# Two Strassen stages of a Hymba step on one Trainium2 core: weight forms and block splits spread between the products

## The chip, the cores and the metric

The kernel runs on one core of a Trainium2 chip. The metric is the device time of one execution in microseconds, the median of several runs. The engines are named as the profile names them: PE (TensorE), DVE (VectorE), ACT (ScalarE), POOL (GpSimd) and SP (SyncE, which here only issues DMAs).

## What is computed

One layer of a decoder: a mixer (gMLP gating beside sliding-window attention), an output projection, and a feed-forward network, over 1024 prompt rows and 32 sample rows of width 1024, all in fp32. The change lies in the feed-forward network, whose hidden width is 4096:

```python
h = rms_norm(x, g_pre_ffn)
f = jnp.einsum('bsf,fd->bsd', jnp.square(jax.nn.relu(jnp.einsum('bsd,df->bsf', h, w_up))), w_down)
return x + rms_norm(f, g_post_ffn)
```

## The kernel before

Every fp32 matrix product is made of three matmuls on a high and a low part of each operand. `split` (L126) makes the parts: ACT casts to fp32r (L128, the high part), DVE subtracts (L129, the low part). A weight that is split lies in a `unit()`, one of 16 buffers.

Both products of the network are Strassen-Winograd products: seven products in place of eight, on sums and differences of blocks. The seven weight operands, the forms, are made by `up_weights` (L888) from two raw loads of 512 KB: four sums on DVE (L900, L901, L904, L906) and seven splits, ten jobs in all, for both stages.

The **up stage** (from about 371 to 750 us) has 16 pairs p of column blocks of the weight, and two groups g of rows (272 and 256 wide). Each (p,g) is a `Quad` (L774) of seven products of twelve matmuls. A turn of the loop at L1062 takes the next quad q and the one before, prev: `q.first()` (products 1 and 2), `prev.third()` (products 4 and 3, then relu, square and four sums on DVE), `prev.stores()` (seven blocks to the DRAM tensor f_d, issued on SP through `load`), then, where prev ends a pair, the raw loads of pair prev.p + 2 and all ten of its weight jobs, and at last `q.second()` (products 6, 5, 7). Products 1, 6, 7, 4 add up in one PSUM bank, A; between them ACT copies A out (`snap`, L801), and the next one waits for that copy. DVE adds the copies to the other banks: L822 or L829 with product 2, L837 with product 7's snap, L844 with product 3. `fo` is the result buffer of a quad (four in the pool `fop`), and is free again when its stores have landed. The raw up weights `rw` have one pair of buffers (`rawp`).

The **down stage** (752 to 1146 us) has eight rounds r of four steps, (r,0,0), (r,0,1), (r,1,0), (r,1,1), for the weight half c and the row group g (L1108). A step makes products 1, 5, 6, 2, 7, 3, 4, each on two banks of PSUM. Products 1, 6, 7, 4 add up in A; ACT copies A to other banks after products 1 and 6 (`fork`, L1130), and after product 5 (D), 2 (C), 7 (E), 3 (B) and 4 (A) `gather` (L1120) adds the banks to accumulators `accD`, `accC`, `accE`, `accB`, `accA`: copies by ACT in r = 0 (L1124), adds by DVE after (L1126). Product 4 goes on in the bank that the gather into accE reads. Blocks come back from f_d by `f_load` (L1039): six loads and splits for each set. Before step (r,0,0) the program has all ten weight jobs of (r,1,.) and the six block splits of the next round's g = 0, before (r,1,0) ten weight jobs, before (r,1,1) six splits.

After that, `combine` (L1209) adds accD to accB and accE for each row group, and `Finish` (L1161) transposes, scales and stores the output.

PE's and SP's order is that of the program. ACT, DVE and POOL are ordered by the scheduler, by its own priorities, and each engine then works through its list in that order; buffers of a pool are reused in turn, and who takes one waits for the last reader of its former content.

Of the kernel before, what the change touches and what calls it, by code (L numbers as in the profile page):

```python
# [8 lines left out]
F32 = mybir.dt.float32  # L9
# [36 lines left out]
def hymba_step(ctx: ExitStack, tc: tile.TileContext, a: dict):  # L46
# [813 lines left out]
    with ExitStack() as pcx:  # L860
# [27 lines left out]
        def up_weights(raws):  # L888
# [3 lines left out]
            def form(src):  # L892
                w = unit()
                split(w[:, 0], w[:, 1], src)
                return w

            ws = {1: form(b11), 2: form(b21)}
            t13 = unit().bitcast(F32)
            t24 = unit().bitcast(F32)
            vec.tensor_tensor(t13[:, 0], b12, b11, ALU.subtract)  # L900
            vec.tensor_tensor(t24[:, 0], b22, t13[:, 0], ALU.subtract)  # L901
            ws[6] = form(t24[:, 0])
            ws[5] = form(t13[:, 0])
            vec.tensor_tensor(t13[:, 1], b22, b12, ALU.subtract)  # L904
            ws[7] = form(t13[:, 1])
            vec.tensor_tensor(t24[:, 1], b21, t24[:, 0], ALU.subtract)  # L906
            ws[4] = form(t24[:, 1])
            ws[3] = form(b22)
            return ws
# [129 lines left out]
    def f_load(fs, pool_=None):  # L1039
        tiles, r, g = fs  # L1040
        n = SUB[g]
        for a0, a1 in ((0, 2), (2, 4), (4, 7)):
            for f, p in zip(tiles, (2 * r, 2 * r + 1)):
                raw = (pool_ or stage).tile([P, D], F32, name="raw")[:, 0:(a1 - a0) * n].rearrange("p (i c) -> p i c", c=n)
                load(raw, f_d[p][g][:, a0:a1])
                split(f[:, a0:a1, 0], f[:, a0:a1, 1], raw)
        return tiles

    def down_weights(r, c, tiles):
        for i, t in enumerate(tiles):  # L1050
            load(t, a["w_down"][2 * r + c, i])
        return up_weights(tiles)
# [9 lines left out]
    prev = q0  # L1062
    for i, (p, g) in enumerate(seq):
        q = Quad(p, g, ws_up[p])
        q.first()
        prev.third()
        flush()
        prev.stores()
        if prev.g == 1:
            del ws_up[prev.p]  # L1070
            if prev.p + 2 < NPAIR:
                ws_up[prev.p + 2] = up_weights(up_raws(prev.p + 2))
# [4 lines left out]
        if i == len(seq) - 2:  # L1077
# [3 lines left out]
            fs0 = f_load(f_tiles(0, 0, 0))  # L1081
        if i == len(seq) - 1:
            wdn0 = down_weights(0, 0, stage_raws())
        q.second()
        prev = q
# [6 lines left out]
    with ExitStack() as pf:  # L1092
# [3 lines left out]
        frp = pf.enter_context(tc.tile_pool(name="frp", bufs=2, reuse_waits="tile"))  # L1096
        rp = pf.enter_context(tc.tile_pool(name="rp", bufs=2, reuse_waits="tile"))
# [10 lines left out]
        def step(r, c, g, fs, ws, inserts=(), renewed=()):  # L1108
            n = SUB[g]
            A, D_, C, B = [[b[:, 0:n] for b in banks[2 * i:2 * i + 2]] for i in range(4)]  # L1110

# [20 lines left out]
            ins = dict(inserts)  # L1132

# [5 lines left out]
            if 0 in renewed:  # L1139
                renew(banks[6:8], ws[1])  # L1140
            fork(C)
            product(5, D_, True)
            gather("D", D_)
            insert(0, 6)
            product(6, A, False)
            if 1 in renewed:
                renew(banks[6:8], ws[1])
            fork(B)
            product(2, C, False)
            gather("C", C)  # L1150
            insert(1, 2)
            product(7, A, False)
            gather("E", A)
            product(3, B, False)
            gather("B", B)
            insert(2, 4)
            product(4, A, False)
            gather("A", A)
            banks[:] = banks[2:4] + banks[0:2] + banks[6:8] + banks[4:6]

        class Finish:  # L1161
# [7 lines left out]
            def half(self, h, bank):  # L1169
                r, t = self.r, self.t  # L1170
                hs = slice(h * 512, (h + 1) * 512)
                if t == NCH:
                    av = rp.tile([P, 4, NS], F32, name="av")
# [7 lines left out]
                junk = rp.tile([P, 512], BF16, name="rl")  # L1181
# [27 lines left out]
        def combine(g):  # L1209
            for k in "BE":  # L1210
                vec.tensor_tensor(gacc(k, g), gacc(k, g), gacc("D", g), ALU.add)  # L1211

        renew(banks[4:8], wdn0[1])
        f_cur = [fs0, f_load(f_tiles(0, 0, 1), frp)]
        w_cur = [wdn0]
        sets = 2
        for r in range(NR):
            f_nxt, w_nxt = [], []

            def prefetch(g):  # L1220
                nonlocal sets
                if r + 1 < NR:
                    f_nxt.append(f_load(f_tiles(0 if sets % 3 < 2 else 1, r + 1, g), frp))
                    sets += 1

            if r + 1 < NR:
                w_cur.append(down_weights(r, 1, stage_raws()))
                prefetch(0)
                step(r, 0, 0, f_cur[0], w_cur[0])
                step(r, 0, 1, f_cur[1], w_cur[0])  # L1230
                w_nxt.append(down_weights(r + 1, 0, stage_raws()))
                step(r, 1, 0, f_cur[0], w_cur[1])
                prefetch(1)
                step(r, 1, 1, f_cur[1], w_cur[1])
            else:
                w_cur.append(down_weights(r, 1, stage_raws()))
                step(r, 0, 0, f_cur[0], w_cur[0])
# [7 lines left out]
                step(r, 1, 0, f_cur[0], w_cur[1])  # L1245
# [119 lines left out]
```

## Time and profile before

| what | value |
| --- | --- |
| three runs | 1163.37, 1170.16 and 1171.62 us, median 1170.16 |
| profiled execution | 1167.12 us |
| its span, first to last instruction | 1165.4 us |
| busy: PE, PE weight loads, DVE, ACT, POOL | 1060.0, 982.7, 833.1, 531.7, 50.8 us |
| mean granted TensorE clock | 0.967 |
| HBM | 126 GB/s over the span |

The span is what the trace covers; the execution's time has 1.7 us around it. An engine's idle time just before an instruction is put down to what ended it, its releaser. A granted clock of 1.00 is 2.4 GHz, 0.50 is 1.2 GHz.

### The profile page before, as it was taken

Reading aid. Unit: us, or ns where it says so; the run is one execution under the profiler, and the core shown is the slowest. Engines: PE = TensorE matmul, PEld = TensorE weight load, DVE = VectorE, ACT = ScalarE, POOL = GpSimd, SP = SyncE. Lnnn points to the kernel's source line nnn. Section 1 sums busy time; section 2 is a strip of 40 time slices with the busy share of each in tenths; the row PEclk is TensorE's granted clock in tenths of the full one; section 3 lists DMA queues with packets and bytes.
Section 4 is the critical chain, followed back from the end, with each engine's and each line's share of the span. In section 5 each row is a group of like instructions: output and inputs, shape, how many; then the busy total and the mean of one; then the engine's idle time right before and its main releaser. Section 6 shows DMA issues by size and latency. Waiting matters only on the chain. (4 is left out here: it accounts for less than half of the span.)

```text
span 1165.4 us, 19447 instructions
## 1 busy us (share of the span) xinstructions
PE 1060.0 (91%) x7443; PEld 982.7 (84%) x7443; DVE 833.1 (71%) x1707; ACT 531.7 (46%) x1184; POOL 50.8 (4%) x77
## 2 busy tenths in 40 slices
PE   7999999999999989999989898899789889898894
PEld 5888777887878979989989897889789889898894
DVE  6678868776678857657665665746877877878657
ACT  6587956664445323223223322367443544444322
POOL 2000003101010000000000000000000000000001
PEclk9999999999999989999999898999899999999997
DMA  8332211245333243343344333645353332533516
GB/s 275 122 100 73 91 38 34 80 154 172 127 109 127 82 140 108 132 140 135 112 139 152 107 127 106 208 144 171 104 187 108 111 127 95 186 101 103 175 39 220
DMA packets 76077, 147.42 MB, mean 127 GB/s; under 512 B 10048, under 2 KB 40224, under 8 KB 75968
## 3 DMA queue, kind: packets, MB, share of 16 engines
q1 hardware_dynamic: 70176, 132.72, 34.8%
q10 hardware_dynamic: 5808, 13.47, 3.0%
q8 instruction: 58, 0.95, 0.3%
q14 instruction: 35, 0.29, 0.1%
HBM read 102.41 MB, written 44.79 MB: 126 GB/s over the span
## 5 line engine op out<-in xcount | busy, mean ns | idle before, releaser
L64 PE MATMUL z<-f,w 128*128 128x272 f32 (+1 forms) x1920 | 263.5, 295 | 39.4 <-DVE accE L1126 21.6
L64 PEld LDWEIGHTS z<-f,w 128*128 128x128 f32 x1920 | 252.2, 198 | 45.0 <-DVE accE L1126 23.0
L64 PE MATMUL z<-w,hT_hi 128*128 128x512 f32 (+1 forms) x768 | 210.2, 380 | 0.4 <-DVE raw L192 0.4
L64 PE MATMUL z<-hT_hi,w 128*128 128x272 f32 (+1 forms) x768 | 153.5, 294 | 11.9 <-ACT w L128 11.3
L64 PEld LDWEIGHTS z<-w,hT_hi 128*128 128x128 f32 x768 | 133.8, 188 | 25.2 <-DVE raw L192 0.8
L64 PEld LDWEIGHTS z<-hT_hi,w 128*128 128x128 f32 x768 | 127.7, 198 | 13.1 <-ACT w L128 11.8
L64 PE MATMUL z<-sg,w 128*128 128x272 f32 (+1 forms) x768 | 109.6, 294 | 17.8 <-ACT s L801 17.7
L64 PE MATMUL z<-w,hT_lo 128*128 128x512 f32 (+1 forms) x384 | 124.5, 378 | 0.0
L64 PEld LDWEIGHTS z<-sg,w 128*128 128x128 f32 x768 | 102.0, 196 | 19.6 <-ACT s L801 19.1
L64 PE MATMUL z<-hT_lo,w 128*128 128x272 f32 (+1 forms) x384 | 112.5, 293 | 0.0
L128 ACT CAST f<-raw 128x544 fp32r<-128x544 f32 (+3 forms) x96 | 67.3, 707 | 96.5 <-DMA raw<-f_d 65.7
L129 DVE TENSOR_TENSOR f<-raw,f 128x544 fp32r<-128x544 f32 (+3 forms) x96 | 75.2, 795 | 42.0 <-ACT f L128 41.6
L64 PE MATMUL t<-f,w 128*128 128x272 f32 (+1 forms) x768 | 104.1, 285 | 0.0
L801 ACT COPY s<-z 128x256 f32<-128x256 f32 (+1 forms) x93 | 35.0, 377 | 143.5 <-PE z L64 133.7
L64 PEld LDWEIGHTS t<-f,w 128*128 128x128 f32 x768 | 97.9, 189 | 0.0
L128 ACT CAST w<-w 128x512 fp32r<-128x512 f32 x128 | 71.0, 617 | 51.2 <-DVE w L901 46.2
L129 DVE TENSOR_TENSOR w<-w 128x512 fp32r<-128x512 f32 x128 | 80.3, 683 | 0.2 <-ACT w L128 0.2
L64 PEld LDWEIGHTS z<-w,hT_lo 128*128 128x128 f32 x384 | 67.6, 188 | 14.0
L1130 ACT COPY t<-z 128x256 f32<-128x256 f32 (+1 forms) x128 | 46.6, 366 | 68.1 <-PE z L64 64.8
L64 PEld LDWEIGHTS z<-hT_lo,w 128*128 128x128 f32 x384 | 76.1, 198 | 0.0
L772 DVE SCALAR_TENSOR_TENSOR fo<-fo 128x544 f32<-128x544 f32 (+1 forms) x64 | 44.9, 702 | 22.1 <-ACT fo L841 21.7
L64 PE MATMUL t<-sg,w 128*128 128x272 f32 (+1 forms) x384 | 52.9, 287 | 1.1 <-DVE fo L822 0.6
(255 smaller groups left out, 1581.7 us busy)
## 6 DMA issues: line engine op xcount, KB each, us to landing
raw<-in_w_down_dram SPq DMA_DIRECT2D x32, 512.0 KB, 5.8
rw<-in_w_up_dram SPq DMA_DIRECT2D x28, 512.0 KB
f_d<-fo SPq DMA_DIRECT2D x64, 136.0 KB, 1.8
raw<-f_d SPq DMA_DIRECT2D x32, 272.0 KB, 3.2
f_d<-fo SPq DMA_DIRECT2D x64, 128.0 KB, 1.8
raw<-f_d SPq DMA_DIRECT2D x32, 256.0 KB
f_d<-raw SPq DMA_DIRECT2D x48, 136.0 KB, 1.8
raw<-f_d SPq DMA_DIRECT2D x16, 408.0 KB, 3.3
```

The source lines that it names most:

```text
L64: tc.keep_in_program_order(pe.matmul(out, lhsT, rhs, start=start, stop=stop, skip_group_check=resumed))
L128: pin(act.copy(hi, src))
L129: pin(vec.tensor_tensor(lo, src, hi.bitcast(F32), ALU.subtract))
L772: vec.scalar_tensor_tensor(f, f, 0.0, f, ALU.max, ALU.mult)
L801: act.copy(s, self.A)
L1130: act.copy(dst[j], A[j])
```

## The change

It does five things. (1) `up_weights` becomes `weight_jobs`, a list of ten jobs (form 1, first sums, form 2, sum, form 6, form 5, sum, form 7, form 4, form 3), and the up loop runs two of them after `q.first()`, two before `q.second()` and two after it. (2) The raw loads of a pair are issued one quad earlier, and ahead of the seven stores of that turn. (3) In the down stage block fetches, block splits and weight jobs are spread over seven slots (`background`) of each step. (4) The raw block buffers `fr` of the down stage are four in place of two. (5) `combine(1)` is cut in two halves, one ahead of the last step.

```diff
-            ws = {1: form(b11), 2: form(b21)}
...
+            return [lambda: form(1, b11), t12, lambda: form(2, b21), t4, lambda: form(6, lambda: tmp["b"][:, 0]),
+                    lambda: form(5, lambda: tmp["a"][:, 0]), t3, lambda: form(7, lambda: tmp["a"][:, 1]),
+                    lambda: form(4, lambda: tmp["b"][:, 1]), lambda: form(3, b22)]
...
+    raws = {2: up_raws(2)}
+    jobs = []
+
+    def work(k):
+        for job in jobs[:k]:
+            job()
+        del jobs[:k]
+
     for i, (p, g) in enumerate(seq):
         q = Quad(p, g, ws_up[p])
         q.first()
+        work(2)
         prev.third()
         flush()
-        prev.stores()
         if prev.g == 1:
             del ws_up[prev.p]
             if prev.p + 2 < NPAIR:
-                ws_up[prev.p + 2] = up_weights(up_raws(prev.p + 2))
+                ws_up[prev.p + 2] = {}
+                jobs += weight_jobs(raws.pop(prev.p + 2), ws_up[prev.p + 2])
+        elif prev.p + 2 < NPAIR and prev.p > 0:
+            raws[prev.p + 2] = up_raws(prev.p + 2)
+        prev.stores()
...
+        work(2)
         q.second()
+        work(2)
         prev = q
...
-        frp = pf.enter_context(tc.tile_pool(name="frp", bufs=2, reuse_waits="tile"))
-        rp = pf.enter_context(tc.tile_pool(name="rp", bufs=2, reuse_waits="tile"))
+        frp = pf.enter_context(tc.tile_pool(name="frp", bufs=4, reuse_waits="tile"))
+        avp = pf.enter_context(tc.tile_pool(name="avp", bufs=2, reuse_waits="tile"))
...
+            def background(i):
+                nonlocal done
+                k = len(jobs) * (i + 1) // 7
+                for job in jobs[done:k]:
+                    job()
+                done = k
...
-                w_cur.append(down_weights(r, 1, stage_raws()))
-                prefetch(0)
-                step(r, 0, 0, f_cur[0], w_cur[0])
-                step(r, 0, 1, f_cur[1], w_cur[0])
-                w_nxt.append(down_weights(r + 1, 0, stage_raws()))
-                step(r, 1, 0, f_cur[0], w_cur[1])
-                prefetch(1)
-                step(r, 1, 1, f_cur[1], w_cur[1])
...
+                step(r, 0, 0, f_cur[0][0], w_cur[0], mix(first, wj[:5]) + fetches(g0[:3]))
+                step(r, 0, 1, f_cur[1][0], w_cur[0],
+                     mix(splits(g0[:3]), wj[5:]) + fetches(g0[3:]) + [wload(r + 1, 0)])
+                wj = weight_jobs(wraw, w_nxt[0])
+                step(r, 1, 0, f_cur[0][0], w_cur[1], mix(splits(g0[3:]), wj[:5]) + fetches(g1[:3]))
+                step(r, 1, 1, f_cur[1][0], w_cur[1],
+                     mix(splits(g1[:3]), wj[5:]) + fetches(g1[3:]) + [wload(r + 1, 1)])
+                late = g1[3:]
...
-        combine(1)
+                combine(1, 0, 2)
+                step(r, 1, 1, f_cur[1][0], w_cur[1], (), [(0, finish(2)), (1, finish(3)), (2, finish(NCH))], True)
+        combine(1, 2, 4)
```

Here `first` is `late`, the last three block splits of the current round's g = 1 (with more in r = 0), `wj` the ten jobs of the next weights, and `mix` takes from two lists in turn.

SP at the start of the up stage, before: the stores of a turn (f_d0_1 is pair 0, g = 1), then the raw loads of pair 2 (rw_4558, rw_4559).

```order
L51 DMA f_d1_0_100<-fo_4223 128x272
L51 DMA f_d0_1_99<-fo_4376 128x256
L51 DMA f_d0_1_99<-raw_4546 128x256 x2
L51 DMA f_d0_1_99<-fo_4377 128x256
L51 DMA f_d0_1_99<-raw_4546 128x256
L51 DMA f_d0_1_99<-fo_4376 128x256
L51 DMA f_d0_1_99<-fo_4377 128x256
L51 DMA rw_4558<-in_w_up_dram 128x1024
L51 DMA rw_4559<-in_w_up_dram 128x1024
L51 DMA f_d1_1_101<-fo_4489 128x256
```

The same place after (rw_4442 and rw_4443 are the raw loads of pair 3):

```order
L51 DMA f_d0_0_98<-fo_4189 128x272
L51 DMA rw_4442<-in_w_up_dram 128x1024
L51 DMA rw_4443<-in_w_up_dram 128x1024
L51 DMA f_d1_0_100<-fo_4226 128x272
L51 DMA f_d1_0_100<-raw_4437 128x272 x2
L51 DMA f_d1_0_100<-fo_4227 128x272
L51 DMA f_d1_0_100<-raw_4437 128x272
L51 DMA f_d1_0_100<-fo_4226 128x272
L51 DMA f_d1_0_100<-fo_4227 128x272
L51 DMA f_d0_1_99<-fo_4380 128x256
```

The loads of pair 3 have moved ahead of the stores of quad (1,0); pair 2's stand still further ahead.

DVE at the same place, before: the last row of post-processing of quad (0,1) (L852), product 7's add of quad (1,1) (L837), then the jobs of pair 2.

```order
L852 TENSOR_TENSOR fo_4376<-fo_4377,raw_4546 128x256
L837 TENSOR_TENSOR fo_4490<-t_4488,s_4627 128x256
L129 TENSOR_TENSOR w_4562<-rw_4558,w_4562 128x512
L129 TENSOR_TENSOR w_4565<-rw_4558,w_4565 128x512
L900 TENSOR_TENSOR w_4568<-rw_4559,rw_4558 128x512
L904 TENSOR_TENSOR w_4568<-rw_4559 128x512
L901 TENSOR_TENSOR w_4569<-rw_4559,w_4568 128x512
```

And after: w_4744 is form 3 of pair 2, the rows from w_4779 on are jobs of pair 3, and L829 and L837 belong to quad (1,1).

```order
L129 TENSOR_TENSOR w_4741<-w_4570,w_4741 128x512
L852 TENSOR_TENSOR fo_4380<-fo_4381,raw_4554 128x256
L129 TENSOR_TENSOR w_4744<-rw_4220,w_4744 128x512
L129 TENSOR_TENSOR w_4779<-rw_4442,w_4779 128x512
L900 TENSOR_TENSOR w_4782<-rw_4443,rw_4442 128x512
L904 TENSOR_TENSOR w_4782<-rw_4443 128x512
L901 TENSOR_TENSOR w_4783<-rw_4443,w_4782 128x512
L129 TENSOR_TENSOR w_4830<-rw_4442,w_4830 128x512
L907 TENSOR_TENSOR w_4783<-rw_4442,w_4783 128x512
L129 TENSOR_TENSOR w_4875<-w_4783,w_4875 128x512
L829 TENSOR_TENSOR fo_4497<-z_4495,s_4511 128x256
L837 TENSOR_TENSOR fo_4498<-t_4496,s_4611 128x256
```

The jobs of pair 2 have moved up into the work of the quad before, and jobs of pair 3, which need rw_4442 and rw_4443, now stand ahead of L829 and L837 of quad (1,1).

DVE in a step (r,0,0) of the down stage, before: the end of the row of jobs (`w`) and block splits (`f`) ahead of the first gathers.

```order
L906 TENSOR_TENSOR w_9890<-raw_9879,w_9890 128x512
L129 TENSOR_TENSOR w_9893<-w_9890,w_9893 128x512
L129 TENSOR_TENSOR w_9896<-w_9889,w_9896 128x512
L129 TENSOR_TENSOR w_9900<-w_9889,w_9900 128x512
L129 TENSOR_TENSOR w_9904<-w_9890,w_9904 128x512
L129 TENSOR_TENSOR w_9907<-raw_9880,w_9907 128x512
L129 TENSOR_TENSOR f_9911<-raw_9916,f_9911 128x2x272
L129 TENSOR_TENSOR f_9910<-raw_9920,f_9910 128x2x272
L1126 TENSOR_TENSOR accD_8322<-z_8325,accD_8322 128x272
L1126 TENSOR_TENSOR accD_8322<-z_8326,accD_8322 128x272
L1126 TENSOR_TENSOR accC_8319<-t_8327,accC_8319 128x272
```

The same step after (the gather is L1168 there):

```order
L129 TENSOR_TENSOR w_9932<-raw_9873,w_9932 128x512
L1168 TENSOR_TENSOR accD_8322<-z_8325,accD_8322 128x272
L1168 TENSOR_TENSOR accD_8322<-z_8326,accD_8322 128x272
L907 TENSOR_TENSOR w_9913<-raw_9873,w_9913 128x512
L129 TENSOR_TENSOR w_9982<-w_9913,w_9982 128x512
L129 TENSOR_TENSOR w_10019<-w_9912,w_10019 128x512
L1168 TENSOR_TENSOR accC_8319<-t_8327,accC_8319 128x272
L129 TENSOR_TENSOR f_9877<-fr_9985,f_9877 128x2x272
L1168 TENSOR_TENSOR accC_8319<-t_8328,accC_8319 128x272
L129 TENSOR_TENSOR w_10053<-w_9912,w_10053 128x512
L1168 TENSOR_TENSOR accE_8321<-z_8323,accE_8321 128x272
L1168 TENSOR_TENSOR accE_8321<-z_8324,accE_8321 128x272
```

Weight jobs and splits now stand between the gathers; fourteen stood ahead of accD before.

## Rows read from the trace of the kernel before

**Rows 1.** Up and down stage: busy us of PE, PEld, DVE, ACT, POOL; clock, DMA.

```profile
371.00:750.00 379.00, 346.30 (x2700) 342.61 (x2698) 252.23 (x487) 116.73 (x259) 1.41 (x2) 0.96 0.39 129
752.00:1146.00 394.00, 353.60 (x2739) 347.24 (x2737) 293.01 (x567) 183.19 (x389) 2.20 (x4) 0.96 0.39 129
```

**Rows 2.** Waits in 371 to 750 us: us in total, times, longest.

```profile
PE z L64 <- ACT s L801: 18.3, 8, 3.7
PE z L64 <- ACT w L128: 11.3, 2, 5.8
...
DVE fo L829 <- DMA f_d<-fo: 5.7, 3, 4.0
```

**Rows 3.** Waits in 752 to 1146 us.

```profile
PE z L64 <- DVE accE L1126: 21.6, 6, 4.0
...
PE z L64 <- DVE accA L1126: 7.9, 5, 6.6
...
PE z L64 <- ACT t L1130: 2.5, 4, 1.1
...
PE z L64 <- ACT accA L1124: 2.2, 2, 1.9
...
PE z L64 <- ACT accE L1124: 1.5, 1, 1.5
```

**Rows 4.** Short stretches of both stages, columns as in Rows 1.

```profile
415.50:422.20 6.70, 3.06 (x12) 2.84 (x13) 3.08 (x5) 1.14 (x2) 0.00 (x0) 0.50 0.51 157
599.80:603.20 3.40, 3.40 (x18) 3.40 (x17) 2.99 (x8) 0.37 (x1) 0.00 (x0) 0.50 0.12 39
603.20:606.60 3.40, 3.40 (x30) 3.40 (x30) 0.00 (x0) 0.67 (x2) 0.00 (x0) 1.00 0.61 209
756.80:760.20 3.40, 3.40 (x16) 3.40 (x17) 1.59 (x3) 1.30 (x4) 0.00 (x0) 0.50 0.45 143
```

**Rows 5.** Timeline 452.5 to 464 us: start, us, instruction, [idle before, releaser].

```profile
452.74 0.87 SPq L51 DMA_DIRECT2D rw<-in_w_up_dram  x2
...
462.98 0.36 ACT L801 COPY s<-z 128x256 f32<-128x256 f32 x1
...
463.39 1.01 PE L64 MATMUL z<-sg,w 128*128 128x256 f32 x3 [2.61 <-ACT s L801]
```

**Rows 6.** Timeline 903 to 914.5 us, a step (r,0,0).

```profile
903.39 1.29 DVE L129 TENSOR_TENSOR w<-raw,w 128x512 fp32r<-128x512 f32 x2 [2.01 <-ACT w L128]
...
904.21 1.03 PE L64 MATMUL z<-f,w 128*128 128x272 f32 x6 [1.01 <-ACT t L1130]
...
905.08 1.67 PE L64 MATMUL t<-f,w 128*128 128x272 f32 x12
...
906.58 1.67 PE L64 MATMUL z<-f,w 128*128 128x272 f32 x12
...
911.92 0.78 DVE L1126 TENSOR_TENSOR accD<-z,accD 128x272 f32<-128x272 f32 x2
...
913.80 1.05 PE L64 MATMUL z<-f,w 128*128 128x272 f32 x3 [4.04 <-DVE accE L1126]
```

**Rows 7.** Timeline 408 to 420 us, the start of the up stage.

```profile
408.56 0.42 DVE L829 TENSOR_TENSOR fo<-z,s 128x256 f32<-128x256 f32 x1 [4.03 <-DMA f_d<-fo]
...
411.74 1.60 PE L64 MATMUL z<-sg,w 128*128 128x256 f32 x12
412.05 0.42 DVE L852 TENSOR_TENSOR fo<-fo,raw 128x256 f32<-128x256 f32 x1
...
414.46 0.88 SPq L51 DMA_DIRECT2D rw<-in_w_up_dram  x2
418.47 1.14 ACT L128 CAST w<-rw 128x512 fp32r<-128x512 f32 x2 [4.72 <-DMA rw<-in_w_up_dram]
...
419.14 0.59 PE L64 MATMUL z<-hT_hi,w 128*128 128x272 f32 x1 [5.80 <-ACT w L128]
```

**Rows 8.** Timeline 1148 to 1150.5 us, behind the last step.

```profile
1148.56 1.20 DVE L1211 TENSOR_TENSOR accB<-accB,accD 128x1024 f32<-128x1024 f32 x1
```

More of the change, by code (lines that the diff above doesn't have):

```diff
@@ L1037, in f_tiles, with f_jobs, one, fetch @@
         return [f_pools[s].tile([P, 7, 2, SUB[0]], F32R, name="f")[:, :, :, 0:n] for _ in range(2)], r, g
-    def f_load(fs, pool_=None):
+    def f_jobs(fs, p_, shape, name):
         tiles, r, g = fs
         n = SUB[g]
[L1042 to L1049, printed above, removed]
+        def one(a0, a1, f, p):
+            raw = []
+            def fetch():
+                raw.append(p_.tile(shape, F32, name=name)[:, 0:(a1 - a0) * n].rearrange("p (i c) -> p i c", c=n))
+                load(raw[0], f_d[p][g][:, a0:a1])
+            def parts():
+                split(f[:, a0:a1, 0], f[:, a0:a1, 1], raw[0])
+            return fetch, parts
+        return [one(a0, a1, f, p) for a0, a1 in ((0, 2), (2, 4), (4, 7)) for f, p in zip(tiles, (2 * r, 2 * r + 1))]
+    def down_load(r, c, tiles):
         for i, t in enumerate(tiles):
             load(t, a["w_down"][2 * r + c, i])
-        return up_weights(tiles)
+        return tiles
     def stage_raws():
@@ L1080, in hymba_step @@
             f_pools.append(pq.enter_context(tc.tile_pool(name="fp", bufs=4, side="right", reuse_waits="tile")))
-            fs0 = f_load(f_tiles(0, 0, 0))
+            fs0 = f_tiles(0, 0, 0)
+            for fetch, parts in f_jobs(fs0, stage, [P, D], "raw"):
+                fetch()
+                parts()
         if i == len(seq) - 1:
-            wdn0 = down_weights(0, 0, stage_raws())
+            wdn0 = up_weights(down_load(0, 0, stage_raws()))
+        work(2)
         q.second()
+        work(2)
         prev = q
@@ new lines, in f_set, with fr_jobs, mix, fetches @@
+        def f_set(i):
+            return f_tiles(0 if i % 3 < 2 else 1, i // 2, i % 2)
+        def fr_jobs(fs):
+            return f_jobs(fs, frp, [P, 3 * SUB[0]], "fr")
+        renew(banks[4:8], wdn0[1])
+        f_cur = [fs0, f_set(1)]
+        w_cur = [wdn0, {}]
+        coming = fr_jobs(f_cur[1])
+        for fetch, _ in coming[0:3]:
+            fetch()
+        late = coming[3:]
+        for fetch, _ in late[0:1]:
+            fetch()
+        wraw = down_load(0, 1, stage_raws())
+        for r in range(NR):
+            last = r + 1 == NR
+            wj = weight_jobs(wraw, w_cur[1])
+            if r == 0:
+                first = [p for _, p in coming]
+                first[1:1] = [coming[4][0]]
+                first[3:3] = [coming[5][0]]
+            else:
+                first = [p for _, p in late]
+            if not last:
+                f_nxt = [f_set(2 * r + 2), f_set(2 * r + 3)]
+                w_nxt = [{}, {}]
+                g0 = fr_jobs(f_nxt[0])
+                g1 = fr_jobs(f_nxt[1])
+                def mix(x, y):
+                    out = []
+                    while x or y:
+                        out += [x.pop(0)] if len(x) >= len(y) and x else [y.pop(0)]
+                    return out
+                def fetches(x):
+                    return [f for f, _ in x]
+                def splits(x):
+                    return [p for _, p in x]
+                def wload(rr, c):
+                    def go():
+                        nonlocal wraw
+                        wraw = down_load(rr, c, stage_raws())
+                    return go
+                step(r, 0, 0, f_cur[0][0], w_cur[0], mix(first, wj[:5]) + fetches(g0[:3]))
[6 more added lines that the diff above has]
+                late = g1[3:]
+                f_cur, w_cur = f_nxt, w_nxt
+            else:
+                step(r, 0, 0, f_cur[0][0], w_cur[0], wj)
```

76 lines of the change are left out of this document (35 added, 41 removed).

## The prediction

> **What bounds the kernel now.** I read the busy times stage by stage first [rows 1]. In the up stage (371 to 750 us) PE is busy for 346.3 of 379 us, in the down stage (752 to 1146 us) for 353.6 of 394. DVE has 252 and 293 us, ACT 117 and 183, the DMA engines a share of 0.39 in both. TensorE sets the pace, and its idle time, 33 and 40 us, is the first thing to be had. The waits say who ends it. In the up stage [rows 2] these are ACT's copies of a running sum (snaps, `s`), 18.3 us in 8 waits, and weight forms that ACT is still casting, 11.3 us in 2. In the down stage [rows 3] they are DVE's adds into accE, 21.6 us in 6 waits (one for each r from 1 to 6), accA 7.9, the forks `t` 2.5, and the copies of r = 0, 2.2 and 1.5: 35.7 together.
>
> Then the clock [rows 4]. From 599.8 us, right behind one of these waits, the granted clock is 0.50 (1.2 GHz) for 3.4 us, and PE, never idle, starts 18 matmuls; in the next 3.4 us, at 1.00 (2.4 GHz), it starts 30. A microsecond of work at half clock so costs (30 - 18)/30 = 0.4 us. The mean granted clock of both stages is 0.96 [rows 1]; with two levels that is (1 - 0.96)/0.5 of each: 30.3 us of the up stage and 31.5 of the down stage at half clock.
>
> Why the waits are there shows where all engines are listed together. Up [rows 5]: the two raw weight loads of a pair are issued at 452.74, behind seven block stores; the ten weight jobs then run in one lump as soon as they land; and the snap that PE has waited for since 460.8 (463.39 less 2.61) comes behind the lump's casts, at 462.98. Down [rows 6]: in step (r,0,0) fourteen weight and block operations stand in a row on DVE from 903.39 to 911.92, 0.61 us each, ahead of the first gather (accD); C and E follow, and product 4, which adds on E's bank, starts at 913.80, 4.04 us late.
>
> **The change, part by part.** PE's order stays as it is, so I follow who comes late to it.
>
> *Up weights in portions, raws a quad earlier.* The same ten jobs now stand in three places of each quad, two at a time, between the snaps. The loads are issued about a quad, 7 products of 1.5 us (905.08 to 906.58 [rows 6]), ahead of the first cast; in the trace issue to first cast takes 4.0 us (414.46 to 418.47 [rows 7]). The casts then lie in ACT's idle time (262 of 379 us), the splits in DVE's. The waits for snaps behind 420 us go: 18.3 less two of 0.6 at the stage's start, 17.1. So does the second wait for a weight form, 11.3 - 5.8 = 5.5.
>
> *The start of the up stage.* Here the change adds a wait on SP, and I expect no gain. Pair 3's second raw takes the buffer that pair 2's form 3 reads. Its load waits for that split, and the seven stores of quad (1,0) stand behind it on SP; for them waits L829 of quad (1,1), which takes their buffer, and behind that stands L837, for which product 3 of (1,1) waits. By rows [rows 7]: L852 of quad (0,1) is at 412.05; four splits stand beside it, so form 3's ends at about 412.5 + 4 x 0.6 = 414.9. With 4.0 to the landing that is 418.9, and six weight operations, L829 and L837, 8 x 0.6 at most, end at 423.7. PE would be there at 417.8 (product 7 ends 1.6 behind 411.74, and three products follow). So 6 us or, with a cast between, 7 in place of the 5.8 at 419.14: I take 6.5, +0.7 (bounds -2 and +3).
>
> *New small waits in the up stage.* With work between the snaps one can be late by a cast, 0.57 us (two in 1.14 [rows 7]). I allow 1.5 us over the stage; the bounds are 0 and the 18.3 of today [rows 2].
>
> *Down stage: jobs in seven slots of each step.* The operations stay: 293 us of DVE over eight r, 36.6 each [rows 1], against PE's 394 less 35.7 idle less 10 for the clock, 348, or 43.5 each. DVE is 84% busy then. By the changed order at most four weight or block operations, 2.4 us, stand between two gathers, and a gather has about two products, 3 us, before its bank is used. Of the 3.7 us of r = 0 I leave 1. For r = 1 to 7 one wait stays, at product 7 of (r,0,0): its fork stands on ACT behind casts that wait for L907. The row nearest to it is that of the forks, 0.6 us on average and 1.1 at most [rows 3]. As DVE has little to spare I take 1.5 us for each r, with bounds of 0.6 and 3. That leaves 1 + 7 x 1.5 = 11.5 of 35.7, and 24.2 go.
>
> *Fetches and four raw block buffers.* The down stage moves the same bytes, at a DMA share of 0.39 [rows 1]. The raw weights are issued a step, 10 us, ahead of their first cast, against 4.0 us for a pair of loads [rows 7]; what a late one costs (0 to 1 us for each r) is inside the bounds above.
>
> One rule speaks against loads ahead of stores. The row is that of 408.56 [rows 7]: L829 started 4.03 us late for a block store, in all 5.7 us in three such waits [rows 2], none of them repeated by PE as a wait of its own. The Trainium skill, "DMA: Bandwidth & Descriptors", section "Issuing engines are not separate DMA queues", says that all DMAs end on the same 16 engines and interleave, so that a pair of loads ahead of the stores slows these. By the rule each pair's stores would land up to 4 us later, and if one of them reached PE in 13 pairs the sum would be 1116; by the row it is nothing. I go by the row; 1116 lies inside the forecast's own range.
>
> *The clock.* Up: of 30.3 us, 6.7 lie about the wait at 419 [rows 4] and stay, and I take 3 as idle inside other waits: 20.6 x 0.4 = 8.2. Down: of 31.5, the 3.4 at 756.8 [rows 4] belong to the change of stages and stay, 3 taken as idle: 25 x 0.4 = 10.0. Both go with the long waits; if they stay, so does this sum (rivals).
>
> *Tail.* Each L1211 behind the last step, 1.20 us [rows 8], becomes half as wide, two times about 0.6 less: -1.2. The other halves lie in idle DVE time of the step before; without that cover they would cost the 1.2 again.
>
> **The sum** is made against the profiled execution, 1167.1 us (span 1165.4 and 1.7 around it): up -17.1 - 5.5 + 0.7 + 1.5 - 8.2 = -28.6; down -24.2 - 10.0 = -34.2; tail -1.2. Together -64.0, so 1103. That execution lies 0.3% below the median of 1170.2 and within the runs, 1163 to 1172, so I set nothing on top. The forecast's own range is 1091 (-2.7 at the start, -1.5 for the small waits, -6.3 for 0.6 at each r, -1.2 more of the idle half clock) to 1118 (+2.3 at the start, +10.5 for 3 at each r, and 1.4 of clock once or twice).
>
> **Rivals.** (a) *One stage is only half cured.* If DVE's queue still brings accE late, the 21.6 us and the forks' 2.5 stay, and with them six stretches of half clock (6 x 1.4 = 8.4). Of the down stage's 34.2 some 12 are left, the total is -42, and the time 1125. For it: DVE at 84%, and raw weights among its gathers. Against: it was one lump that made the row of fourteen. The mirror case, snaps late although the lump is cut (17.1 and 6 of clock stay), gives 1126; both together 1148.
>
> (b) *Slower: the jam at the start comes again in every pair.* There is one pair of raw buffers, with loads ahead of stores on SP. If at each p the load waits for the form 3 before it, the seven stores are late, L829's buffer is not free, and product 3 waits 6.5 us with one stretch of half clock, 1.4: 13 pairs x 7.9 = 103, and 1206. For it speaks L829's wait at 408.56 [rows 7]. Against it: in the later pairs of the changed order the forms of the pair before end about a quad ahead of the load. It is decided at 64.0/13 = 4.9 us for each pair; from there on the kernel is slower than before.
>
> (c) *It does not do what it says.* ACT's and DVE's order is the scheduler's, which could draw the jobs together again; all but the tail stays, 1166. Against it stands the changed order itself.
>
> **How the numbers follow.** The forecast has 0.63, (a) in one stage 0.20, in both 0.04, (b) 0.08, (c) 0.05. A measurement of this kernel can tell about 1% from no change, 1158.5 to 1181.9 us: faster is the forecast with (a), 0.87; within 1% is (c), 0.05; slower is (b), 0.08. The range goes from 1089, just under the forecast's own, to 1140, past the one-stage rivals; both stages, (b) and (c), 0.17, stay out.
>
> **What would show it.** Right: no wait of PE for `s` above 1 us between 430 and 720 us, none for accE above 2 us, a granted clock of 0.98 or more in both stages, and one wait of 6 to 7 us near 420 us, ended by L837 in place of a cast. Wrong: accE or the snaps at 3 to 4 us in each r or pair (a), or L829 and L837 behind `f_d` stores in each pair (b).

## The result, and the profile after

The changed kernel takes 1093.07 us (median of four runs, 1089.6 to 1095.5) against 1169.45 for the kernel before (median of four, 1163.4 to 1171.6): a ratio of 0.9353, 95% interval 0.9307 to 0.9398. The forecast was 1103, with a range of 1089 to 1140. The profiled execution took 1091.66 us, its span is 1089.9.

Where the 75.5 us of span went shows best between three marks on PE: its first up matmul, its first matmul on f (the first of the down stage), and its last one. The times are read off the timelines of both kernels, the forecast stands beside them:

| stretch, us | before | after | difference | forecast |
| --- | --- | --- | --- | --- |
| up to the first up matmul | 371.6 | 373.0 | +1.4 | 0 |
| up stage with the change of stages | 380.5 | 354.5 | -26.0 | -28.6 |
| down stage | 392.7 | 343.0 | -49.7 | -34.2 |
| behind the last down matmul | 20.6 | 19.4 | -1.2 | -1.2 |

These are single executions. The changed kernel profiled a second time (e9 below) has 371.9 us up to the first up matmul and 352.7 in the up stage, so the first row is about as large as that scatter, and differences of less than some 5 us in a stage are not to be relied on.

Busy times between the same marks, columns as in [rows 1]: up and down stage before, then after.

```profile
371.60:752.10 380.50, 347.62 (x2702) 343.67 (x2701) 253.09 (x488) 117.33 (x259) 1.41 (x2) 0.96 0.39 130
752.10:1144.80 392.70, 352.35 (x2731) 346.29 (x2729) 291.81 (x565) 182.81 (x388) 2.20 (x4) 0.96 0.39 129
373.00:727.50 354.50, 338.73 (x2701) 334.36 (x2700) 247.10 (x487) 115.08 (x256) 1.41 (x2) 0.99 0.42 138
727.50:1070.50 343.00, 337.81 (x2730) 335.45 (x2729) 289.94 (x567) 178.88 (x389) 2.20 (x4) 0.99 0.44 149
```

PE's idle time in the down stage is 343.0 - 337.8 = 5.2 us, where it was 392.7 - 352.4 = 40.3. Its busy time fell too, by 14.5 us for the same matmuls, with the granted clock at 0.99 in place of 0.96; how much of that is the clock is taken up below. DVE does the same 290 us of work, now in 343 us, 85% busy.

What PE waits for in the up stage after (371 to 750 us), against [rows 2]; the first row is DVE's wait for stores:

```profile
DVE fo L829 <- DMA f_d<-fo: 18.9, 6, 4.8
...
PE z L64 <- ACT s L801: 8.4, 11, 1.7
...
PE t L64 <- DVE fo L837: 4.5, 1, 4.5
```

And all that it waits for in the down stage after (727.5 to 1070.5 us), against [rows 3]:

```profile
PE z L64 <- ACT w L128: 1.5, 1, 1.5
PE z L64 <- DVE w L1228: 1.1, 1, 1.1
PE t L64 <- DVE w L1228: 0.9, 1, 0.9
PE z L64 <- DVE accA L1168: 0.9, 1, 0.9
PE z L64 <- ACT accA L1166: 0.4, 1, 0.4
PE z L64 <- DVE w L129: 0.3, 1, 0.3
```

No row of accE is left, and none of the forks. Why, a step (r,0,0) shows, with what comes ahead of it (timeline 849 to 869 us; [rows 6] are the same place before). Before, the step began at 899.2, and its raw weights were issued at:

```profile
896.01 0.90 SPq L51 DMA_DIRECT2D raw<-in_w_down_dram  x2
```

After:

```profile
850.21 0.90 SPq L51 DMA_DIRECT2D raw<-in_w_down_dram  x2
...
856.37 0.62 ACT L128 CAST w<-raw 128x512 fp32r<-128x512 f32 x1 [2.14 <-DMA raw<-in_w_down_dram]
...
857.02 0.69 DVE L129 TENSOR_TENSOR w<-raw,w 128x512 fp32r<-128x512 f32 x1 [0.31 <-ACT w L128]
...
861.20 0.78 DVE L1168 TENSOR_TENSOR accD<-z,accD 128x272 f32<-128x272 f32 x2
861.90 0.68 DVE L907 TENSOR_TENSOR w<-raw,w 128x512 f32<-128x512 f32 x1
862.50 1.29 DVE L129 TENSOR_TENSOR w<-w 128x512 fp32r<-128x512 f32 x2
863.70 0.43 DVE L1168 TENSOR_TENSOR accC<-t,accC 128x272 f32<-128x272 f32 x1
...
865.63 0.78 DVE L1168 TENSOR_TENSOR accE<-z,accE 128x272 f32<-128x272 f32 x2
...
866.93 2.27 PE L64 MATMUL z<-f,w 128*128 128x272 f32 x17
```

The step begins at 857.9. Its weight jobs begin on DVE at 857.0, 0.9 us ahead of the step; before, they began at 903.39 in a step that had begun at 899.2, 4.2 us into it. The raws were issued 7.7 us ahead of the step, before 3.2 us. Now three weight operations stand between accD and accC, accE is done at 866.4, and product 4 starts without a wait.

The place in the up stage where no gain was expected (timeline 405 to 426 us, against [rows 7]):

```profile
409.09 6.23 SPq L51 DMA_DIRECT2D rw<-in_w_up_dram  x2
...
414.28 1.28 DVE L129 TENSOR_TENSOR w<-rw,w 128x512 fp32r<-128x512 f32 x2
...
417.89 1.45 SPq L51 DMA_DIRECT2D f_d<-fo  x3
...
419.03 0.69 DVE L900 TENSOR_TENSOR w<-rw 128x512 f32<-128x512 f32 x1 [3.47 <-DMA rw<-in_w_up_dram]
...
422.65 0.42 DVE L829 TENSOR_TENSOR fo<-z,s 128x256 f32<-128x256 f32 x1
```

SP stands at the two loads from 409.09 to 415.32, until form 3 of the pair before has been split; the seven stores of quad (1,0) come behind it, the last three from 417.89 to 419.34; L900 waits 3.47 us for the second raw, L829 and L837 stand behind it, and PE's `PE t L64 <- DVE fo L837` of 4.5 us ends at 423.45.

### The profile page after: what moved, and what is told of

The parts are those of the page before. It is cut to its first block, busy times and chain, and to the rows that moved or that the text cites. A ratio compares the mean times of both kernels' runs of the same rounds, so it can differ in the third digit from the quotient of the medians.

```text
span 1089.9 us, 19465 instructions
## 1 busy us (share of the span) xinstructions
PE 1037.8 (95%) x7443; PEld 963.9 (88%) x7443; DVE 825.2 (76%) x1709; ACT 526.6 (48%) x1184; POOL 52.6 (5%) x77
## 5 line engine op out<-in xcount | busy, mean ns | idle before, releaser
L64 PE MATMUL z<-f,w 128*128 128x272 f32 (+1 forms) x1920 | 249.9, 287 | 4.2 <-ACT w L128 1.5
L64 PEld LDWEIGHTS z<-f,w 128*128 128x128 f32 x1920 | 241.3, 190 | 6.1 <-ACT w L128 1.8
L64 PE MATMUL z<-w,hT_hi 128*128 128x512 f32 (+1 forms) x768 | 211.0, 381 | 0.4 <-DVE raw L192 0.4
L64 PEld LDWEIGHTS z<-w,hT_hi 128*128 128x128 f32 x768 | 134.4, 189 | 25.3 <-DVE raw L192 0.8
L64 PE MATMUL z<-hT_hi,w 128*128 128x272 f32 (+1 forms) x768 | 149.1, 287 | 3.2 <-ACT s L801 3.0
L64 PEld LDWEIGHTS z<-hT_hi,w 128*128 128x128 f32 x768 | 122.6, 189 | 5.3 <-ACT s L801 5.2
L64 PE MATMUL z<-w,hT_lo 128*128 128x512 f32 (+1 forms) x384 | 124.8, 379 | 0.0
L128 ACT CAST w<-w 128x512 fp32r<-128x512 f32 x128 | 74.7, 619 | 97.1 <-DVE w L901 46.3
L64 PE MATMUL z<-sg,w 128*128 128x272 f32 (+1 forms) x768 | 105.9, 287 | 5.5 <-ACT s L801 5.4
L64 PE MATMUL z<-hT_lo,w 128*128 128x272 f32 (+1 forms) x384 | 109.4, 285 | 0.0
L64 PEld LDWEIGHTS z<-sg,w 128*128 128x128 f32 x768 | 98.9, 190 | 7.2 <-ACT s L801 7.2
L64 PE MATMUL t<-f,w 128*128 128x272 f32 (+1 forms) x768 | 104.3, 285 | 0.0
L64 PEld LDWEIGHTS t<-f,w 128*128 128x128 f32 x768 | 98.3, 189 | 0.0
L129 DVE TENSOR_TENSOR w<-w 128x512 fp32r<-128x512 f32 x128 | 84.7, 687 | 13.3 <-ACT w L128 12.8
L128 ACT CAST f<-fr 128x512 fp32r<-128x512 f32 (+3 forms) x90 | 62.6, 709 | 61.9 <-PE z L64 32.5
L129 DVE TENSOR_TENSOR f<-fr,f 128x512 fp32r<-128x512 f32 (+3 forms) x90 | 70.3, 793 | 16.7 <-ACT f L128 16.0
L64 PEld LDWEIGHTS z<-w,hT_lo 128*128 128x128 f32 x384 | 67.9, 189 | 14.1
L64 PEld LDWEIGHTS z<-hT_lo,w 128*128 128x128 f32 x384 | 72.9, 190 | 0.0
L64 PE MATMUL t<-sg,w 128*128 128x272 f32 (+1 forms) x384 | 54.0, 291 | 4.5 <-DVE fo L837 4.5
L64 PEld LDWEIGHTS t<-sg,w 128*128 128x128 f32 x384 | 50.7, 194 | 4.7 <-DVE fo L837 4.7
```

What stands on the lines that cost most here:

```text
L64: tc.keep_in_program_order(pe.matmul(out, lhsT, rhs, start=start, stop=stop, skip_group_check=resumed))
L128: pin(act.copy(hi, src))
L129: pin(vec.tensor_tensor(lo, src, hi.bitcast(F32), ALU.subtract))
```

## The experiments

The question after this result: the change does two things at once in each stage. It cuts the lump (the ten weight jobs in one place) into portions, and it gives their inputs a longer lead (time between a load's issue and the work that needs it). Theory of the prediction: the lump was the cause. Rival: the late loads were. The stretches in this section are taken between the marks of the table above, in one profiled execution of each kernel; ratios are to the kernel before on the same chip.

**Each stage by itself.** In `e1_up_only` the up loop is the changed one, with the down stage of before; `e2_down_only` is the other half. All diffs of this section are against the changed kernel, cut to their core; `...` marks what is left out.

```diff
 e1
-        frp = pf.enter_context(tc.tile_pool(name="frp", bufs=4, reuse_waits="tile"))
+        frp = pf.enter_context(tc.tile_pool(name="frp", bufs=2, reuse_waits="tile"))
...
-                step(r, 0, 0, f_cur[0][0], w_cur[0], mix(first, wj[:5]) + fetches(g0[:3]))
+                w_cur.append(down_weights(r, 1, stage_raws()))
+                prefetch(0)
+                step(r, 0, 0, f_cur[0], w_cur[0])
...
 e2
-        work(2)
...
+        prev.stores()
         if prev.g == 1:
...
-                jobs += weight_jobs(raws.pop(prev.p + 2), ws_up[prev.p + 2])
+                ws_up[prev.p + 2] = up_weights(up_raws(prev.p + 2))
```

> Only the up stage is changed; the down stage and the tail are those of before. Theory (each stage gains for itself, since PE's order is one chain): from the first up matmul to the first down matmul the changed kernel took 354.5 us where before took 380.5, so 26 less: 1143.5 us, ratio 0.978; the down stage keeps its 392.7 us and its accE waits. Rival (the stages share the gain, the clock or the DMA queues carry it over): the up stage's part comes out at less than half, above 1156, or the down stage gets shorter by over 5 us too.

> Only the down stage, the four block buffers and the halved combine are changed; the up stage is that of before. Theory: the down stage falls from 392.7 to 343 us and the tail by 1.2, 1118.5 us, ratio 0.956, with up waits and half clock as before. Rival (part of the down stage's gain comes from weights and blocks that the changed up stage had ready earlier): the down stage stays above 355 us.

Measured: e1 1143.07 us, ratio 0.9734 (0.9665 to 0.9803), up stage 357.6, down stage 395.0. e2 1120.96, ratio 0.9572 (0.9508 to 0.9636), up stage 380.9, down stage 344.6. Each stage keeps its own waits where it wasn't changed, as these rows show, first of e1 (728 to 1125 us), then of e2 (371 to 750 us):

```profile
PE z L64 <- DVE accE L1165: 21.8, 6, 4.2
```

```profile
PE z L64 <- ACT s L801: 17.3, 8, 3.5
PE z L64 <- ACT w L128: 11.4, 2, 6.5
```

Within their intervals the gains add up (0.9734 x 0.9572 = 0.9317, beside 0.9353) and neither stage feeds the other; the rival of a shared gain falls. The up stage alone is the less certain of the two, with an interval that reaches to 0.980.

**Buffers and tail.** `e3_two_fr` and `e4_combine_late`:

```diff
 e3
-        frp = pf.enter_context(tc.tile_pool(name="frp", bufs=4, reuse_waits="tile"))
+        frp = pf.enter_context(tc.tile_pool(name="frp", bufs=2, reuse_waits="tile"))
 e4
-                combine(1, 0, 2)
...
-        combine(1, 2, 4)
+        combine(1)
```

> The changed kernel with two raw block buffers in place of four. Theory (the spreading of the jobs made the gain, the buffers only let fetches run ahead): within 5 us of the changed kernel, 1093 to 1098. Rival (the four buffers made it): three fetches a step wait for splits, SP holds the weight loads behind them, the forms come late and accE with them; 3 us of wait and 1.5 of clock for each of seven r, about 1125.

> The changed kernel with combine(1) whole and behind the last step again. Theory: two adds of 1.20 us in place of two of about 0.6 behind the last step, the wait of PE's first transposes of accB grows from 2.15 to about 3.3 us and the end comes 1.2 us later; no time tells that from nothing, the trace does. Rival: the halves ahead of the last step cost as much as they save; the stretch from the last down matmul to the end stays at 19.4 us.

e3 took 1107.1 us, ratio 0.9439 (0.9387 to 0.9492), between both expectations. Its down stage is 358.6 us, 15.6 more than in the changed kernel. PE's longest wait in sum there (728 to 1086 us), and the busy times of the stage:

```profile
PE z L64 <- DVE accE L1168: 8.8, 16, 1.5
```

```profile
727.40:1086.00 358.60, 341.53 (x2731) 335.07 (x2729) 289.85 (x568) 182.41 (x389) 2.19 (x4) 1.00 0.44 142
```

And SP at the same place as above, ahead of and in the step (r,0,0) that begins at 863.2 (timeline 850 to 876 us):

```profile
856.68 6.69 SPq L51 DMA_DIRECT2D fr<-f_d  x4
...
863.43 1.27 SPq L51 DMA_DIRECT2D raw<-in_w_down_dram  x2
```

With two buffers SP stands at four fetches for 6.69 us, and the weight loads behind them go out 0.2 us into the step, not 7.7 us ahead of it; their first cast is at 868.25, 5 us into it. The jobs are as spread in the program as in the changed kernel, and accE is late again, though by 1.5 us at most, and no stretch of half clock follows. Part of the down stage's gain is the lead, and the buffers give it. That the weights and not the late blocks make accE late is read from this step, where weight operations stand ahead of it; no run has late weights alone.

e4 took 1093.27 us in its one run. The trace: an add of full width (that into accE takes 1.21),

```profile
1074.75 1.20 DVE L1257 TENSOR_TENSOR accB<-accB,accD 128x1024 f32<-128x1024 f32 x1
```

a wait of PE for accB of 3.9 us in place of 2.15, and 20.5 us behind the last down matmul in place of 19.4. By one trace of each, the halved combine is worth 1.1 us, as its term had it; no time tells that from nothing.

**Portions or lead, up stage.** `e5_lump_early_loads` puts the ten jobs in one place of the code and leaves the early loads; `e6_portions_late_loads` leaves the portions and puts the loads back behind the stores of the later turn; `e7_loads_behind` keeps both, and moves the loads of each turn from ahead of its stores to behind them.

```diff
 e5
-                jobs += weight_jobs(raws.pop(prev.p + 2), ws_up[prev.p + 2])
+                lump = weight_jobs(raws.pop(prev.p + 2), ws_up[prev.p + 2])
...
         prev.stores()
+        if prev.g == 1:
+            for job in lump:
+                job()
 e6
-    raws = {2: up_raws(2)}
+    raws = {}
...
-                jobs += weight_jobs(raws.pop(prev.p + 2), ws_up[prev.p + 2])
-        elif prev.p + 2 < NPAIR and prev.p > 0:
-            raws[prev.p + 2] = up_raws(prev.p + 2)
         prev.stores()
+        if prev.g == 1 and prev.p + 2 < NPAIR:
+            jobs += weight_jobs(up_raws(prev.p + 2), ws_up[prev.p + 2])
 e7
-        elif prev.p + 2 < NPAIR and prev.p > 0:
-            raws[prev.p + 2] = up_raws(prev.p + 2)
         prev.stores()
+        if prev.g == 0 and prev.p + 2 < NPAIR and prev.p > 0:
+            raws[prev.p + 2] = up_raws(prev.p + 2)
```

> The changed kernel, but all ten up weight jobs of a pair stand in one place again (behind the stores of the turn, in the code); the loads stay a quad early and ahead of the stores. Theory (the lead of the loads freed the snaps: by the order of this kernel the scheduler draws the lump apart as soon as the raws count as there): the up stage stays within 5 us of the changed kernel's 354.5, 1090 to 1098. Rival (the portions did it): the snaps are 2 to 3 us late in each of seven pairs as before, with the clock, 17 + 8 us, about 1118.

> The changed kernel with the jobs in portions, but the two raw loads again behind the seven stores of the turn in which the pair before ends, as in the kernel before. Theory (lead of the loads): casts wait for the DMA again, snaps behind them are late, PE's waits for s are at least 10 us in sum and the up stage at least 362 us, 1101 or more. Rival (portions): up stage within 5 us of 354.5. In both the wait near 423 us changes: the jam of pair 3's load ahead of the stores isn't there.

> The changed kernel with each pair's raw loads still a quad early, but behind the seven stores of that turn. Theory (the wait of 4.54 us near 423 us is the one that the loads ahead of the stores made, and their place is worth nothing elsewhere): the wait and its half clock go, 4.5 + 1.5, snaps wait as long as now (8.4 us): about 1087. Rival (in each pair the load is late by the stores' issue, some 3 us, and a cast stands ahead of a snap by that): snap waits of 15 us or more, 1095 or above.

e5: 1090.44 us, ratio 0.9338 (0.9292 to 0.9384), up stage 351.7. e6: 1105.12, ratio 0.9452 (0.9404 to 0.9501), up stage 363.9. e7: 1082.39, ratio 0.9251 (0.9197 to 0.9306), up stage 347.3. PE's waits in the up stage (371 to 726 us) of e5:

```profile
PE z L64 <- ACT s L801: 5.0, 8, 1.7
PE t L64 <- DVE fo L837: 4.7, 1, 4.7
```

of e6:

```profile
PE z L64 <- ACT w L128: 10.2, 2, 5.5
PE z L64 <- ACT s L801: 9.9, 11, 1.9
```

Portions in the code are worth nothing that these times tell where the loads are early: the scheduler draws the lump apart by itself, as DVE shows in e5 (timeline 500 to 531 us), where three weight operations stand between the adds L837 and L829 of two quads. In the kernel before, eleven run from 457.24 to 464.6 with one other among them.

```profile
507.24 0.41 DVE L837 TENSOR_TENSOR fo<-t,s 128x256 f32<-128x256 f32 x1
507.57 1.28 DVE L129 TENSOR_TENSOR w<-w 128x512 fp32r<-128x512 f32 x2
508.77 0.68 DVE L904 TENSOR_TENSOR w<-rw 128x512 f32<-128x512 f32 x1
511.23 0.44 DVE L829 TENSOR_TENSOR fo<-z,s 128x272 f32<-128x272 f32 x1 [1.78 <-DMA f_d<-fo]
```

Late loads leave something of the old waits even with portions: both waits for a weight form (10.2 us) are back, and the up stage is 9.4 us longer than the changed one, though the jam near 423 us isn't there. Still, e6's up stage is 16.6 us shorter than before, so the portions are worth about that where the loads are late (nearer 13 by the medians: 1169.4 - 1105.1 = 64.3, less the 50.9 of down stage and tail; the profiled execution was the quickest of its four). Either cures most of the snaps; the lead cures the forms as well. So the lump need not be cut in the code of the up stage. Whether a lump that stays whole on DVE would hurt there with early loads, no run shows, as the scheduler didn't keep it whole.

In e7 PE's wait near 423 us is gone, as the theory had it, but the load is no earlier (timeline 405 to 426 us):

```profile
409.56 0.89 SPq L51 DMA_DIRECT2D f_d<-fo  x2
...
410.79 7.30 SPq L51 DMA_DIRECT2D rw<-in_w_up_dram  x2
...
411.45 0.42 DVE L829 TENSOR_TENSOR fo<-z,s 128x256 f32<-128x256 f32 x1
...
416.67 0.42 DVE L837 TENSOR_TENSOR fo<-t,s 128x256 f32<-128x256 f32 x1
...
421.82 0.69 DVE L900 TENSOR_TENSOR w<-rw 128x512 f32<-128x512 f32 x1 [3.53 <-DMA rw<-in_w_up_dram]
```

SP stands at the loads for 7.30 us, no less than in the changed kernel, and L900 waits 3.53 us for its raw. Two other things differ. The stores of quad (1,0), which L829's buffer waits for, are all issued by 410.45, where the changed kernel issues the last of them at 419.34; and L829 and L837 now come ahead of L900 on DVE. It is likely that the scheduler had put them behind it because their buffer's stores came behind the loads, but that is a reading, and no run separates the two. What PE waited for was not the load itself but what stood behind it, on SP and on DVE.

**The lump, down stage.** `e10_down_lump` keeps buffers, fetches and loads, and puts all ten weight jobs and the step's splits in the first slot of (r,0,0) and (r,1,0).

```diff
-                k = len(jobs) * (i + 1) // 7
+                k = max(k0, len(jobs) * (i + 1) // 7)
...
-                step(r, 0, 0, f_cur[0][0], w_cur[0], mix(first, wj[:5]) + fetches(g0[:3]))
+                step(r, 0, 0, f_cur[0][0], w_cur[0], wj + first + fetches(g0[:3]), k0=10 + len(first))
```

> The changed kernel with all ten down weight jobs (and the splits of the step) in the first slot of steps (r,0,0) and (r,1,0); buffers, fetches and loads as changed. By its order eight weight operations stand in a row ahead of accD in step (r,0,0), ten with two behind accA, where before had fourteen. Theory (the row of operations ahead of the gathers makes accE late): 4.0 less four times 0.6, so waits for accE of 1.5 to 2.5 us in each of six r, the down stage 10 to 16 us longer, and up to 9 more where the clock falls: 1104 to 1118. Rival (four buffers and earlier fetches cured it): within 3 us of the changed kernel, 1090 to 1096.

It took 1099.4 us, ratio 0.9408 (0.9359 to 0.9456), with 349.6 us of down stage: 6.6 more, between the two expectations, and not where the theory had it. PE's waits (727 to 1077 us) name the forks and the start, not accE:

```profile
PE z L64 <- ACT t L1172: 2.7, 8, 0.5
PE z L64 <- ACT accA L1166: 2.5, 1, 2.5
```

DVE in the step that begins at 860.9 (timeline 850 to 875 us):

```profile
859.71 0.69 DVE L129 TENSOR_TENSOR w<-raw,w 128x512 fp32r<-128x512 f32 x1
...
866.90 0.68 DVE L129 TENSOR_TENSOR w<-raw,w 128x512 fp32r<-128x512 f32 x1
867.50 0.78 DVE L1168 TENSOR_TENSOR accD<-z,accD 128x272 f32<-128x272 f32 x2
...
868.90 0.78 DVE L1168 TENSOR_TENSOR accE<-z,accE 128x272 f32<-128x272 f32 x2
```

The lump is there, but it starts 1.2 us ahead of the step, where before it started 4.2 us into it, and accE is done 8.8 us into the step, before product 4 (the sixth product has ended 9 us in). So of the down stage's 49.7 us a lump by itself is worth 6.6, in which the single waits are 2.5 us at most; with the lead gone and the jobs spread (e3) it is 15.6. The two do not add up to 49.7: the long waits and the falling clock are there only with both a late start and a lump, in the kernel before and in e1 (395.0 us). The lump of e10 is shorter, though: nine weight operations run between accA and accD here, where fourteen operations stood ahead of accD before, so what the whole row costs with early loads isn't measured.

**Toward a better kernel.** Four kernels on one chip, where times compare directly: the changed kernel again (`e9`), e7 again (`e11`), `e8_pair3_behind`, which has pair 3's loads alone behind the stores, and `e12_early_down`, which adds to e7 an earlier load of the first down weights.

```diff
 e8
-        elif prev.p + 2 < NPAIR and prev.p > 0:
+        elif prev.p + 2 < NPAIR and prev.p > 1:
             raws[prev.p + 2] = up_raws(prev.p + 2)
         prev.stores()
+        if prev.g == 0 and prev.p == 1:
+            raws[3] = up_raws(3)
 e12
         if i == len(seq) - 2:
+            wraw = down_load(0, 0, [rawp.tile([P, D], F32, name="rw") for _ in range(2)])
...
-            wdn0 = up_weights(down_load(0, 0, stage_raws()))
+            wdn0 = up_weights(wraw)
```

> The changed kernel as it is, beside the next three on one chip. Both theories: 1093, ratio 0.935 to before.

> The kernel with each pair's raw loads a quad early but behind the stores, once more, beside the changed kernel. Theory (loads ahead of the stores cost the jam near 423 us and make stores and with them L829 late in other pairs; behind them they cost nothing): 7 to 11 us below the changed kernel, ratio about 0.927. Rival (the 10 us of the first comparison were scatter between chips): within 4 us of the changed kernel.

> The changed kernel with pair 3's loads alone behind the stores of quad (1,0); pairs 4 to 15 stay ahead. Theory (what the loads behind the stores gain is the one jam at the start, 4.5 us of wait and 1.5 of half clock): 1087, and snap waits as in the changed kernel, about 8 us. Rival (part of the gain is that later stores go out first): no wait near 423 us, but 3 to 5 us slower than with all loads behind.

> The kernel with the loads behind the stores, and the first down stage weights loaded one quad earlier too, into the raw up buffers that are free by then. Theory (the lead of loads is what sets these waits, at the change of stages too): the waits of 4.19, 1.59 and 0.67 us at 720 to 727 us and two stretches of half clock (about 3 us) go, 6 to 9 us below the kernel without it, about 1075. Rival (those casts wait for free weight units, which the last up products hold): within 3 us of it.

| kernel | us, median of six | ratio to before, 95% interval | up stage, us |
| --- | --- | --- | --- |
| e9, changed | 1091.04 | 0.9312 (0.9271 to 0.9354) | 352.7 |
| e11, loads behind stores | 1081.04 | 0.9221 (0.9185 to 0.9258) | 342.5 |
| e8, pair 3's loads behind | 1084.38 | 0.9249 (0.9210 to 0.9289) | 345.0 |
| e12, early down weights too | 1082.63 | 0.9236 (0.9199 to 0.9273) | 348.0 |

The gain of loads behind stores is there again, 10 us, with intervals that do not meet: e11 beats both kernels. Two thirds of it, 6.7 us, e8 has too, by the one place near 423 us. The last 3 us are less certain, as those intervals overlap; but PE's waits for snaps (371 to 730 us) are 6.8 us in 10 waits in e8 and 3.2 in 3 in e11, which points to the other pairs, the rival of e8. The up stages of this table do not rank the kernels: e8's profiled execution was the quickest of its six, 4.5 us below their median, and the kernel of e11 and e7 has 342.5 and 347.3.

e12 is a miss. Against e7 the waits at the change of stages (4.19, 1.59 and 0.67 us; in e11 1.84, 2.19 and 0.72) went, as expected, but one of about the same size came in their place (timeline 710 to 724 us):

```profile
714.91 0.68 DVE L129 TENSOR_TENSOR w<-w 128x512 fp32r<-128x512 f32 x1
...
716.12 0.42 DVE L837 TENSOR_TENSOR fo<-t,s 128x256 f32<-128x256 f32 x1
...
716.59 2.93 PE L64 MATMUL t<-sg,w 128*128 128x256 f32 x12 [4.15 <-DVE fo L837]
```

With the earlier weights, jobs stand ahead of the last quad's L837, and PE waits 4.15 us for it. The rival's figure, within 3 us of e11, came true; its reason (free weight units) isn't what the trace shows.

## Why the prediction was right, and where it was off

The forecast, 1103, lies 10 us above what was measured, and the range holds it, near its lower end. The waits to be had, who ends them and the place of the one new wait were read rightly. The cause was half of it: the prediction had the early loads of the up stage in its account, but laid the gain on cutting the lump, in the down stage above all, and gave the four buffers no term. There was some luck in the sum: most of the long waits go by either way, so it came near though only one of the two was priced. By its own steps:

- *Up weights*: the waits of 2.3 to 3.7 us for snaps went, and the second wait for a form, as forecast. The reason given, portions between the snaps, was half of it: by e5 early loads are enough, as the scheduler then spreads the jobs itself.
- *The start of the up stage*: the mechanism came as forecast, SP, L829, L837 and product 3, at 4.5 us where 6.5 was taken (its lower bound was 5.8 - 2 = 3.8). The eight operations stand behind the landing as counted, and took 4.4 us (419.03 to 423.4) for 4.8; the landing took 3.7 for 4.0 (415.32 to 419.03), and the further cast, for which 6 was made 6.5, didn't come. The larger part of the miss is PE itself: it came at 423.45 - 4.54 = 418.9, not at the 417.8 that was worked out.
- *New small waits*: 1.2 us that stay (read as two at the stage's start; one, at 744.9, is at its end) and 1.5 new ones were taken; `s` has 8.4 us in 11 waits, 5.7 more. This is the largest term that was too good.
- *Down stage, what is left*: 11.5 us was taken; of the waits summed there accA has 0.9 and 0.4 left, 1.3, and none is at the place named (the fork ahead of product 7). The step that was off is the choice of 1.5 us for each r because DVE has little to spare. DVE is 85% busy, as worked out, and PE hardly waits for it: in e3, at the same work of DVE, late loads bring accE's waits back.
- *Fetches and four raw block buffers*: a late load was to cost 0 to 1 us for each r, inside the bounds above. By e3 the two further buffers are worth 15.6 us, some 2 for each r. The raw weights were taken to be issued 10 us ahead of their first cast; it was 6.2 (850.21 to 856.37).
- *The clock*: 18.2 us was taken, in the up stage 8.2 and in the down stage 10.0. PE's busy time, between the marks, fell by 8.9 and 14.5. The amount of half clock was right in the down stage: the clock intervals of the traces add up to 32 us before and 6.6 after, 25 less, as taken. The price of 0.4 may be low; behind the wait at 423.45, 15 matmuls start in 3.3 us, then 29 in 3.4, which makes some 0.47. At that price 25 us give 12. The rest of the 14.5 is not the clock: e3 has a clock of 1.00, and PE is busy for 341.5 us, 3.7 more than in the changed kernel. PE's busy time so seems to hold part of the waits too. That of the weight loads (second column) does not: it fell by 10.8 us, near the clock's 12, and is the same in e3 as in the changed kernel.

```profile
423.50:426.80 3.30, 3.30 (x15) 3.30 (x16) 3.30 (x8) 0.62 (x1) 0.00 (x0) 0.50 0.13 43
426.90:430.30 3.40, 3.40 (x29) 3.40 (x29) 2.41 (x5) 0.39 (x1) 0.00 (x0) 1.00 0.26 81
```

- *Tail*: -1.2 forecast, -1.2 in the table, 1.1 by e4.
- *Rival (b)*, the jam in every pair: it came once. L829's wait for block stores rose from 5.7 to 18.9 us, but PE did not take it up. With the loads behind the stores it rose further, to 33.3 us in e11, and that kernel is the quickest, so what the prediction feared of loads ahead of stores, slower stores in each pair that reach PE, no run shows. The Trainium skill, "DMA: Bandwidth & Descriptors", section "Issuing engines are not separate DMA queues", says that DMAs run on the same 16 engines and interleave, whichever engine started them; what loads and stores cost each other by that, no run here measures.
- *Its signs*: no wait for accE is left, and the clock is 0.99 in both stages. The wait near 420 us is 4.5 us in place of 6 to 7, and three waits for `s` between 430 and 720 us are just above 1 us (1.08, 1.26 and 1.12 at 514.0, 547.4 and 612.1).

In sum the down stage came out 15.5 us better than forecast, 10.2 by the waits and the rest by PE's busy time (4.5 more than was taken) and small waits that the prediction did not sum. The up stage came out 2.6 worse: 5.7 by the small waits, less 2.0 at its start and smaller terms. With 1.4 lost ahead of the first up matmul that makes 11.5, which is what lies between the forecast and the profiled execution.

## What to carry to other kernels

When a lump of side work makes the main engine wait, look first at when its inputs land: the lump of the down stage, begun 5 us earlier, cost 6.6 us, where the stage before lost 49.7, and in the up stage the scheduler drew the lump apart once its loads were early. Ask what stands ahead of its loads on the issuing queue; two more block buffers were worth 15.6 us here, and the step of e3 shown above says for the weight loads behind their fetches. And where a scheduler orders an engine, the order of loads and stores in the program moves what is queued on the others: read that list before blaming a transfer.

## What the runs showed that was not expected

The clock followed waits of like length in two ways. In e2 a wait of 2.35 us that ended at 463.6 was followed by a stretch at 1.2 GHz, one of 2.45 at 693.6 was not. In e3, from 736 us on, sixteen waits for accE of up to 1.5 us left the clock at 2.4 GHz to the end of the down stage. But in the changed kernel two waits of 1.51 and 0.30 us at 731.9 and 732.8, just behind another such stretch, were followed by one at 734.1. So by these rows a wait of 2 to 3 us may cost its own length or 1.6 us more (an estimate, 0.47 x 3.4), and no length of a single wait says which.
